# Hybrid GLA/SSD/PEER block: opening products half a round earlier, the sums' copies in another tag, and two of three passes fused in the later part of the first expert matrix

## The chip, the core and the metric

The kernel runs on one core of a Trainium2 chip: TensorE (PE, with its weight loads PEld), VectorE (DVE), ScalarE (ACT), GpSimd (POOL) and SyncE (SP), whose queue issues the large weight loads. The metric is the device time of one execution in microseconds, the median of several runs. Times inside a run come from one profiled execution.

## The reference, cut to what matters

```python
mod_x = split(silu(c) @ w_ada + b_ada, 6)            # and mod_c from c_ctx
hc = modulate(rmsnorm(ctx, norm1_w), mod_c[0], mod_c[1])
hx = modulate(rmsnorm(x, norm1_w), mod_x[0], mod_x[1])
core_c, states = branch_core(hc, 1, p, None)          # h @ w_in, then GLA and SSD scans
core_x, _ = branch_core(hx, rows, p, states)
x = x + mod_x[2] * branch_out(core_x, p)
hx2 = modulate(rmsnorm(x, norm2_w), mod_x[3], mod_x[4])
x = x + mod_x[5] * peer(hx2, peer_wq, peer_keys, peer_u, peer_v)
return rmsnorm(x, final_norm_w)
# peer: scores -> top 16 of 16384 experts per head -> softmax gates;
# act = gelu(t @ u[idx].T), y = (act * gate) @ v[idx]
```

256 latent and 256 context tokens, width 2048, one layer, everything in float32. The kernel computes the expert part densely: all 16384 rows of u against all 256 tokens, a gate matrix that is zero but for the chosen experts, and all rows of v.

## The kernel before

Every large product is done in split precision: a weight tile of 128 x 1024 arrives as `raw`, ScalarE copies it to `hi` (rounded) and VectorE computes `lo = raw - hi`; the activations are held as a pair hi/lo too. A product of one 128 x 128 slice is then three TensorE passes: Whi with the hi activations, Whi with their lo, Wlo with their hi (`mm3`, L328 to L330). `Stream` runs this supply from one plan for the whole kernel. `get` hands out the next pair, and before it does, `ahead` issues the loads up to `loads` items ahead on SyncE's queue and the splits up to `splits` ahead. There are three raw buffers (`loads - splits`) and four buffers each of hi and lo (`splits + 1`), from the first item to the last.

**The opening** (list `START`, loop at L397). The first 16 of the 24 pieces of 512 columns of the ada product stand in 8 rounds c, each of four pieces `("ada", c, i)` (`ada_piece`, 8 matmuls on four column groups, L263), whose two tiles of 512 KB each come over SyncE's queue too (`board`, up to 7 aboard, in buffers `raw0` and `s4`). After the fourth piece `ada_out` copies the sums to SBUF (ScalarE, L269; the copy is a tile of tag `s4`, five buffers, that also hold two of every seven ada tiles and two K tiles), some steps later turns them with `sel2` (TensorE, L274) and adds the bias. `h_pair(c)` then makes two slices of the modulated, normed input, hi and lo (VectorE, ScalarE). With two slices of h ready, TensorE can do the halves of v (`v_part`, L336 to L338, 12 matmuls of 512 columns each), of the low-rank and dt columns ("ld", L426 to L428, 6 matmuls each), and from round 5 a k product of 24. In round c stand v and ld of pair c - 2, four to five steps one after another between the pieces, and h of pair c - 1 behind the second piece. The engines run their queues in the order in which the code was written out; nothing reorders them.

**The first head.** Then come units of weight columns, each pass followed by `tick`, which moves every background generator by one `yield`. `gla(hd)` is one: the exponentials of a direction (`exps`), their products with Q and K (`prods`, VectorE L555 to L561), the diagonal products on TensorE (`diag`, L568), and so on. The dt stage runs on VectorE in the same stretch.

**The last sum of squares.** After the output projection, `stats` sums the squares of x1 on TensorE (L1135), and four filling ada pieces (L263) follow; the sum goes through Ln and Exp into `rs2`, and h2hi and h2lo are made slice by slice.

**The experts.** `u_tile(b, i)` multiplies a tile of 128 experts of u with h2: two gets of 8 slices each, into half a PSUM bank; every second tile Gelu reads the bank (L1374). 14 blocks of 4 tiles run alone, beside the routing. From then on each tile of the remaining 18 blocks (b of 14 to 31, `BACK = 14`) is followed by a group of v products (L1497 to L1499, 24 matmuls of 512 columns), whose sums VectorE adds to `yacc` (L1506).

Of the kernel before, what the change touches and what calls it, by code (L numbers as in the profile page):

```python
# [10 lines left out]
F32 = mybir.dt.float32  # L11
F32R = mybir.dt.float32r
U32 = mybir.dt.uint32
AF = mybir.ActivationFunctionType
OP = mybir.AluOpType
# [13 lines left out]
class Stream:  # L29
# [10 lines left out]
    def _load(self, i):  # L40
        t = self.pool.tile([P, 1024], F32, name="raw", tag="raw", bufs=self.loads - self.splits)
        self.nc.sync.dma_start(t, self.plan[i])
        self.raw[i] = t

    def _split(self, i):
        t = self.raw.pop(i)
        hi = self.pool.tile([P, 1024], F32R, name="hi", tag="hi", bufs=self.splits + 1)
        lo = self.pool.tile([P, 1024], F32R, name="lo", tag="lo", bufs=self.splits + 1)
        self.nc.scalar.activation(hi, t, AF.Copy)  # L49
        self.nc.vector.tensor_sub(lo, t, hi.bitcast(F32))  # L50
        self.done[i] = (hi, lo)
# [43 lines left out]
def hybrid_block_kernel(ctx, tc, A, out):  # L95
# [8 lines left out]
    st = Stream(nc, streams, 6, 3)  # L104

    def mmbank(shape=(P, 512)):
        return psum.tile(list(shape), F32, name="mm", tag="mm", bufs=4)
# [45 lines left out]
    START = []  # L153
    for c in range(10):
        todo = [("v", c - 2, 0), ("ld", c - 2, 0), ("v", c - 2, 1), ("ld", c - 2, 1)] if c > 1 else []
        if 4 < c < 9:
            todo.append(("k", c - 5, 0))
        for i in range(8):
            if c < 8 and i % 2:
                START.append(("ada", c, i // 2))  # L160
                if not c:
                    START.append(("norm", i // 2, 0))
            if i == 3 and 0 < c < 9:
                START.append(("h", c - 1, 0))
            if todo:
                START.append(todo.pop(0))

# [163 lines left out]

    def v_part(pv, W2, k, j):
        Whi, Wlo = W2
        for tb in range(4):
            tok = slice(P * tb, P * tb + P)
            mm_(pv[tb], Hhi[:, k, tok], Whi[:, j, :], start=k == 0, stop=False)  # L336
            mm_(pv[tb], Hhi[:, k, tok], Wlo[:, j, :], start=False, stop=False)  # L337
            mm_(pv[tb], Hlo[:, k, tok], Whi[:, j, :], start=False, stop=k == KT - 1)  # L338
# [57 lines left out]
    ada_sb = lambda: w4.tile([P, 512], F32, name="s4", tag="s4", bufs=5)  # L396
    plr = pdt = None  # L397
    Kt = {a: w4.tile([P, 2, 512], F32, name="s4", tag="s4", bufs=5) for a in range(2)}
    for k, a, b in START:
# [29 lines left out]
        else:  # L429
            pk = scbank()  # L430
            mm3(pk, st.get(), 0, 8, Hhi, Hlo, CT, True, True)
            later.append(lambda a=a, pk=pk: nc.scalar.activation(Kt[a // 2][:, a % 2], pk, AF.Copy))
        step()
    es_x.close()
    wk = es_w.enter_context(tc.tile_pool(name="wk", bufs=1, reuse_waits="tile"))
    st.limit = st.side = None
    SZ = {"s1": 256, "s2": 512, "s4": 1024}
# [84 lines left out]
    def gla(hd):  # L522
# [51 lines left out]
        yield  # L574
        diag(0)
        prods(1)
        yield
        yield
        diag(1)
# [577 lines left out]
    stats(*prev)  # L1157
    for i in range(FILL):
        ada_piece(i, fill[2 * i:2 * i + 2])
    bg.insert(0, ada_out(23))  # L1160
# [5 lines left out]
    h2hi = h2p.tile([P, KT, T], F32R, name="h2hi")  # L1166
    h2lo = h2p.tile([P, KT, T], F32R, name="h2lo")
# [192 lines left out]
    def u_tile(b, i):  # L1360
        nonlocal started
        if i % 2 == 0:
            u_tile.ps = mmbank((P, 2, 256))
        ps = u_tile.ps
        for h in range(2):
            mm3(ps[:, i % 2], st.get(), 8 * h, 8, h2hi, h2lo, slice(0, 256), h == 0, h == 1)
            if not started and not bg:
                bg.append(bg_route)
                started = True
            tick()  # L1370
        if i == 0:
            ACT_[b] = ap_.tile([P, 4, 256], F32, name="act", tag="act", bufs=BACK + 2)
        if i % 2:
            nc.scalar.activation(ACT_[b][:, i - 1:i + 1], ps, AF.Gelu)  # L1374
# [208 lines left out]
```

## Time and profile before

| | us |
|---|---|
| median of 3 runs | 3626.37 |
| lowest, highest | 3626.19, 3629.07 |
| the profiled execution | 3628.86 |
| its span, first to last instruction | 3627.1 |

Of the span TensorE is busy 3546.5 us (98%), VectorE 2368.4 (65%), ScalarE 1665.6 (46%). A matmul's busy time is longer than its distance from the next, since matmuls are pipelined; so the distance between starts says what one costs. PEclk is the clock that TensorE was granted: 1.0 is 2.4 GHz, and where the mean of a stretch is lower, part of it ran at 1.2 GHz. A wait is put down to the instruction that ended it.

### The profile page before, as it was taken

What the parts mean: (1) busy time and instruction counts of PE and PEld (TensorE: products, weight loads), DVE (VectorE), ACT (ScalarE), POOL (GpSimd) and SP (SyncE); (2) the same over time, 40 slices, a digit from 0 to 9 for tenths busy, and PEclk for the clock granted to TensorE, in tenths of its full rate; (3) what the DMA queues carried; (4) which work ended last, traced back from release to release, by engine and by line L of the source; (5) the groups of instructions that cost most, each with busy time, mean ns of one, the idle gap of its engine ahead of it and who ended that gap; (6) DMA issues with size and microseconds to landing.
All of it is one profiled execution on the core that took longest, in us unless ns stands there. A gap on an engine that the chain in (4) does not pass through costs nothing.

```text
span 3627.1 us, 58908 instructions
## 1 busy us (share of the span) xinstructions
PE 3546.5 (98%) x23679; PEld 3186.4 (88%) x23679; DVE 2368.4 (65%) x3569; ACT 1665.6 (46%) x2225; POOL 370.6 (10%) x424
## 2 busy tenths in 40 slices
PE   5989999999999999999998999999999999999998
PEld 2688899988888888999998999999999999998886
DVE  3375565777878777655545787875555555556777
ACT  2254444445555555654433446464444444444344
POOL 0000000000000000110002016360000000000004
PEclk8999999999999999999999999999999999999999
DMA  8644555655665565567666557677666666666774
GB/s 304 230 140 142 172 170 179 208 170 189 210 206 184 176 191 174 167 230 245 193 209 218 172 182 203 195 208 221 198 198 197 198 197 198 198 198 206 240 228 144
DMA packets 214145, 715.39 MB, mean 197 GB/s; under 512 B 24688, under 2 KB 24832, under 8 KB 213360
## 3 DMA queue, kind: packets, MB, share of 16 engines
q1 hardware_dynamic: 188928, 625.04, 53.5%
q0 software_dynamic: 24944, 86.59, 8.7%
q8 instruction: 186, 3.05, 0.3%
q14 instruction: 87, 0.71, 0.1%
HBM read 679.93 MB, written 31.60 MB: 196 GB/s over the span
## 4 chain that ended last, share of the span: by engine, by line
PE 92%; DVE 4%; DMA 2%; ACT 1%; issue 1%; POOL 0%; DVEq 0%; SPq 0%; ACTq 0%; POOLq 0%
PE mm L328 20%; PE mm L330 20%; PE mm L329 19%; PE mm L1498 6%; PE mm L1497 6%; PE mm L1499 6%; PE mm L336 2%; PE sc L1304 2%; PE mm L337 2%; PE mm L338 2%; DVE lo L50 1%; PE sc L875 1%; PE ad L263 1%; PE sc L615 1%; PE sc L808 1%
## 5 line engine op out<-in xcount | busy, mean ns | idle before, releaser
L50 DVE TENSOR_TENSOR lo<-raw,hi 128x1024 fp32r<-128x1024 f32 x996 | 1234.3, 1246 | 1011.8 <-ACT hi L49 1003.5
L49 ACT ACTIVATE hi<-raw 128x1024 fp32r<-128x1024 f32 x996 | 1046.0, 1058 | 1383.5 <-PE mm L329 624.5
L328 PE MATMUL mm<-Hhi,hi 128*128 128x256 f32 (+1 forms) x2272 | 737.6, 325 | 1.4 <-ACT hi L49 1.4
L330 PE MATMUL mm<-Hhi,lo 128*128 128x256 f32 (+1 forms) x2272 | 724.7, 319 | 4.0 <-DVE lo L50 4.0
L329 PE MATMUL mm<-Hlo,hi 128*128 128x256 f32 (+1 forms) x2272 | 724.2, 319 | 0.0
L328 PE MATMUL mm<-h2hi,hi 128*128 128x256 f32 x2304 | 657.7, 285 | 0.0
L329 PE MATMUL mm<-h2lo,hi 128*128 128x256 f32 x2304 | 653.1, 283 | 2.5 <-DVE h2lo L1175 2.5
L330 PE MATMUL mm<-h2hi,lo 128*128 128x256 f32 x2304 | 652.6, 283 | 0.0
L328 PEld LDWEIGHTS mm<-Hhi,hi 128*128 128x128 f32 x2272 | 435.4, 192 | 37.0 <-issue 5.3
L330 PEld LDWEIGHTS mm<-Hhi,lo 128*128 128x128 f32 x2272 | 435.2, 192 | 34.4 <-DVE lo L50 5.0
L329 PEld LDWEIGHTS mm<-Hlo,hi 128*128 128x128 f32 x2272 | 435.7, 192 | 30.3 <-issue 1.9
L329 PEld LDWEIGHTS mm<-h2lo,hi 128*128 128x128 f32 x2304 | 442.4, 192 | 6.2 <-DVE h2lo L1175 3.1
L328 PEld LDWEIGHTS mm<-h2hi,hi 128*128 128x128 f32 x2304 | 442.1, 192 | 4.1 <-ACT h2hi L1172 0.8
L330 PEld LDWEIGHTS mm<-h2hi,lo 128*128 128x128 f32 x2304 | 442.1, 192 | 0.0
L1498 PE MATMUL mm<-lo,ph 128*128 128x512 f32 x1024 | 406.1, 397 | 5.7 <-DVE lo L50 5.7
L1497 PE MATMUL mm<-hi,ph 128*128 128x512 f32 x1024 | 406.5, 397 | 0.0
L1499 PE MATMUL mm<-hi,pl 128*128 128x512 f32 x1024 | 405.1, 396 | 0.0
L1498 PEld LDWEIGHTS mm<-lo,ph 128*128 128x128 f32 x1024 | 193.0, 188 | 49.5 <-DVE lo L50 7.2
L1499 PEld LDWEIGHTS mm<-hi,pl 128*128 128x128 f32 x1024 | 193.1, 189 | 46.3
L1497 PEld LDWEIGHTS mm<-hi,ph 128*128 128x128 f32 x1024 | 193.2, 189 | 42.8
L330 PE MATMUL mm<-yh,lo 128*128 128x256 f32 x768 | 217.3, 283 | 1.0 <-DVE lo L50 1.0
L328 PE MATMUL mm<-yh,hi 128*128 128x256 f32 x768 | 217.1, 283 | 0.0
(337 smaller groups left out, 4556.1 us busy)
## 6 DMA issues: line engine op xcount, KB each, us to landing
raw<-in_w_f_dram SPq DMA_DIRECT2D x288, 512.0 KB, 3.7
raw<-in_u_dram SPq DMA_DIRECT2D x256, 512.0 KB, 4.1
raw<-in_v_dram SPq DMA_DIRECT2D x256, 512.0 KB, 4.1
ride<-in_w_ada_dram SPq DMA_DIRECT2D x240, 256.0 KB, 3.9
raw<-in_w_so_dram SPq DMA_DIRECT2D x64, 512.0 KB, 4.2
raw<-in_w_ada_dram SPq DMA_DIRECT2D x45, 512.0 KB, 7.3
raw<-in_w_v_dram SPq DMA_DIRECT2D x32, 512.0 KB, 3.6
s<-cum_d POOLq DMA_DIRECT2D x64, 256.0 KB, 6.1
```

What stands on the lines that cost most here:

```text
L49: self.nc.scalar.activation(hi, t, AF.Copy)
L50: self.nc.vector.tensor_sub(lo, t, hi.bitcast(F32))
L328: mm_(ps, Whi[:, j, :], hi[:, k, tok], start=start and j == 0, stop=False)
L329: mm_(ps, Whi[:, j, :], lo[:, k, tok], start=False, stop=False)
L330: mm_(ps, Wlo[:, j, :], hi[:, k, tok], start=False, stop=stop and j == n - 1)
L336: mm_(pv[tb], Hhi[:, k, tok], Whi[:, j, :], start=k == 0, stop=False)
L337: mm_(pv[tb], Hhi[:, k, tok], Wlo[:, j, :], start=False, stop=False)
L338: mm_(pv[tb], Hlo[:, k, tok], Whi[:, j, :], start=False, stop=k == KT - 1)
L1304: mm_(pg[:, j], o1[:, j], o2[:, j], start=True, stop=True)
L1497: mm_(ps[t, i], ghi, Whi, start=j == 0 and k == 0, stop=False)
L1498: mm_(ps[t, i], ghi, Wlo, start=False, stop=False)
L1499: mm_(ps[t, i], glo, Whi, start=False, stop=j == 1 and k == 1)
```

## The change

Five things are changed. In the opening, v and ld of pair c - 1 are put into the list behind the third piece of round c, h of pair c - 1 behind its first piece; leftover steps follow one or two at a time, and the last k product stands last. During the opening the stream loads 5 and splits 2 items ahead instead of 6 and 3, with the same numbers of buffers, and the copy of the sums takes a buffer of tag `sq1`, which the first norm has used before. In the first head, one more empty step stands before each diagonal product. The last `stats` stands behind the third of the four filling pieces. And from block 14 on a tile of u is done by `mm2`: h2hi and h2lo lie side by side in one tile `h2`, Whi multiplies both in one pass of 512 columns, Wlo the hi half in one of 256, into a whole bank, and VectorE adds the two halves of the bank before Gelu.

```diff
@@ class Stream
-        t = self.pool.tile([P, 1024], F32, name="raw", tag="raw", bufs=self.loads - self.splits)
+        t = self.pool.tile([P, 1024], F32, name="raw", tag="raw", bufs=3)
...
-        hi = self.pool.tile([P, 1024], F32R, name="hi", tag="hi", bufs=self.splits + 1)
-        lo = self.pool.tile([P, 1024], F32R, name="lo", tag="lo", bufs=self.splits + 1)
+        hi = self.pool.tile([P, 1024], F32R, name="hi", tag="hi", bufs=4)
+        lo = self.pool.tile([P, 1024], F32R, name="lo", tag="lo", bufs=4)
...
-    st = Stream(nc, streams, 6, 3)
+    st = Stream(nc, streams, 5, 2)
...
-    START = []
+    START, todo = [], []
     for c in range(10):
-        todo = [("v", c - 2, 0), ("ld", c - 2, 0), ("v", c - 2, 1), ("ld", c - 2, 1)] if c > 1 else []
-        if 4 < c < 9:
-            todo.append(("k", c - 5, 0))
-        for i in range(8):
-            if c < 8 and i % 2:
-                START.append(("ada", c, i // 2))
-                if not c:
-                    START.append(("norm", i // 2, 0))
-            if i == 3 and 0 < c < 9:
+        for i in range(4):
+            if c < 8:
+                START.append(("ada", c, i))
+            if c == 0:
+                START.append(("norm", i, 0))
+            if i == 0 and 0 < c < 9:
                 START.append(("h", c - 1, 0))
-            if todo:
-                START.append(todo.pop(0))
+            if i == 2 and 0 < c < 9:
+                todo += [("v", c - 1, 0), ("ld", c - 1, 0), ("v", c - 1, 1), ("ld", c - 1, 1)]
+                if c > 4:
+                    todo.append(("k", c - 5, 0))
+            for _ in range(2 if len(todo) > 4 else 1):
+                if todo:
+                    START.append(todo.pop(0))
+    START += todo
...
+    def mm2(ps, W2, h0, x, start, stop):
+        Whi, Wlo = (w.rearrange("p (k f) -> p k f", f=P) for w in W2)
+        for j in range(8):
+            k = h0 + j
+            last = stop and j == 7
+            for w in (Wlo, Whi) if last else (Whi, Wlo):
+                if w is Whi:
+                    mm_(ps, w[:, j, :], x[:, k], start=start and j == 0, stop=last)
+                else:
+                    mm_(ps[:, 0:256], w[:, j, :], x[:, k, 0], start=False, stop=False)
...
-    ada_sb = lambda: w4.tile([P, 512], F32, name="s4", tag="s4", bufs=5)
+    ada_sb = lambda: xp.tile([P, 512], F32, name="sq1", tag="sq1", bufs=3)
...
+            continue
+        while later:
+            later.pop(0)()
         step()
...
+    st.loads, st.splits = 6, 3
@@ gla
         yield from exps(1)
         yield
+        if hd == 0:
+            yield
         diag(0)
         prods(1)
         yield
         yield
+        if hd == 0:
+            yield
         diag(1)
...
-    stats(*prev)
     for i in range(FILL):
         ada_piece(i, fill[2 * i:2 * i + 2])
+        if i == 2:
+            stats(*prev)
...
-    h2hi = h2p.tile([P, KT, T], F32R, name="h2hi")
-    h2lo = h2p.tile([P, KT, T], F32R, name="h2lo")
+    h2 = h2p.tile([P, KT, 2, T], F32R, name="h2")
+    h2hi, h2lo = h2[:, :, 0], h2[:, :, 1]
@@ u_tile
+        wide = b >= BACK
+        if wide:
+            ps = mmbank()
...
+            if wide:
+                mm2(ps, st.get(), 8 * h, h2, h == 0, h == 1)
...
+        a = ACT_[b][:, i - 1:i + 1]
+        if wide:
+            nc.vector.tensor_reduce(ACT_[b][:, i], ps.rearrange("p (s t) -> p t s", s=2), axis=AX.X, op=OP.add)
         if i % 2:
-            nc.scalar.activation(ACT_[b][:, i - 1:i + 1], ps, AF.Gelu)
+            nc.scalar.activation(a, a if wide else ps, AF.Gelu)
```

The order of the instructions at three places follows, of before and of the changed kernel apart. Line numbers of the changed kernel are its own (L263 is L266 there, L555 L575).

SyncE's queue in rounds 1 and 2 of the opening, before. `raw<-in_w_v_dram`, `in_w_ld_dram` and `in_w_f_dram` are items of the stream (v, ld, k), all others tiles of the ada matrix, in order of their pieces:

```order
L42 DMA raw<-in_w_v_dram 128x1024
L42 DMA raw<-in_w_ld_dram 128x1024
L42 DMA raw<-in_w_v_dram 128x1024
L64 DMA s_256<-in_w_ada_dram 128x1024
L64 DMA s_258<-in_w_ada_dram 128x1024
L64 DMA raw_269<-in_w_ada_dram 128x1024
L64 DMA raw_271<-in_w_ada_dram 128x1024
L64 DMA raw_288<-in_w_ada_dram 128x1024
L64 DMA raw_290<-in_w_ada_dram 128x1024
L64 DMA raw_296<-in_w_ada_dram 128x1024
L64 DMA s_298<-in_w_ada_dram 128x1024
L42 DMA raw<-in_w_f_dram 128x1024
```

The same place in the changed kernel:

```order
L42 DMA raw<-in_w_v_dram 128x1024
L42 DMA raw<-in_w_ld_dram 128x1024
L64 DMA s_250<-in_w_ada_dram 128x1024
L64 DMA s_252<-in_w_ada_dram 128x1024
L64 DMA raw_274<-in_w_ada_dram 128x1024
L64 DMA raw_276<-in_w_ada_dram 128x1024
L64 DMA raw_282<-in_w_ada_dram 128x1024
L64 DMA raw_284<-in_w_ada_dram 128x1024
L42 DMA raw<-in_w_v_dram 128x1024
L64 DMA raw_308<-in_w_ada_dram 128x1024
L64 DMA s_310<-in_w_ada_dram 128x1024
L42 DMA raw<-in_w_v_dram 128x1024
```

Two instead of three items stand ahead of the two `s` tiles of round 1's last piece, and the following items come one by one between the ada tiles.

VectorE in the first head, before: the products of direction 0 (L555 to L561), the small factors of direction 1 (L534 to L536), splits (`lo`), the products of direction 1:

```order
L558 TENSOR_TENSOR s_1562<-s_1562,s_154 128x512
L559 TENSOR_TENSOR s_1565<-s_1565,s_154 128x256
L561 TENSOR_SCALAR s_1566<-s_1563,s_1557 128x128 x2
L534 TENSOR_SCALAR s_1659<-s_1173 128x2x2
L535 TENSOR_SCALAR s_1659<-s_1173 128x2x2
L536 TENSOR_SCALAR s_1659<-s_1173 128x2
L50 TENSOR_TENSOR lo<-raw,hi 128x1024 x2
L555 TENSOR_TENSOR s_1665<-s_1665,s_1455 128x512
```

The same place in the changed kernel:

```order
L578 TENSOR_TENSOR s_1562<-s_1562,s_154 128x512
L579 TENSOR_TENSOR s_1565<-s_1565,s_154 128x256
L581 TENSOR_SCALAR s_1566<-s_1563,s_1557 128x128 x2
L554 TENSOR_SCALAR s_1659<-s_1172 128x2x2
L555 TENSOR_SCALAR s_1659<-s_1172 128x2x2
L556 TENSOR_SCALAR s_1659<-s_1172 128x2
L50 TENSOR_TENSOR lo<-raw,hi 128x1024 x3
L575 TENSOR_TENSOR s_1665<-s_1665,s_1455 128x512
```

One split more stands ahead of the products of direction 1; on TensorE four passes of 24 instead of three stand between the dt stage's transposes and the first diagonal product, three instead of two ahead of the second.

VectorE at a tile of u in the late blocks, before, between two sums of v (`yacc`); in the second group of each block the gates of the next one (L1395, L1398) stand between too:

```order
L1506 TENSOR_TENSOR yacc<-yacc,mm 128x512 x2
L50 TENSOR_TENSOR lo<-raw,hi 128x1024 x4
L1506 TENSOR_TENSOR yacc<-yacc,mm 128x512 x2
L50 TENSOR_TENSOR lo<-raw,hi 128x1024 x2
L1395 TENSOR_TENSOR act<-act,Gb 128x1024
```

The same place in the changed kernel:

```order
L50 TENSOR_TENSOR lo<-raw,hi 128x1024 x2
L1407 TENSOR_REDUCE act<-mm 128x256
L50 TENSOR_TENSOR lo<-raw,hi 128x1024 x2
L1541 TENSOR_TENSOR yacc<-yacc,mm 128x512 x2
L50 TENSOR_TENSOR lo<-raw,hi 128x1024 x2
L1407 TENSOR_REDUCE act<-mm 128x256
L1430 TENSOR_TENSOR act<-act,Gb 128x1024
```

The addition of the two halves of the bank stands behind the second split of each tile and ahead of the splits of the v items.

## Rows read from the trace of the kernel before

**Rows 1.** The page: span, TensorE's busy time with its count, and the chain that ended last by engine.

```profile
span 3627.1 us, 58908 instructions
...
PE 3546.5 (98%) x23679; PEld 3186.4 (88%) x23679; DVE 2368.4 (65%) x3569; ACT 1665.6 (46%) x2225; POOL 370.6 (10%) x424
...
PE 92%; DVE 4%; DMA 2%; ACT 1%; issue 1%; POOL 0%; DVEq 0%; SPq 0%; ACTq 0%; POOLq 0%
```

**Rows 2.** The table by stage: stretch, length, then busy us (instructions) of PE, PEld, DVE, ACT, POOL, the granted clock, the DMA engines' busy share and GB/s. The first 150 us, and a stretch of the late blocks.

```profile
0.00:150.00 150.00, 112.86 (x544) 60.50 (x545) 51.01 (x87) 39.22 (x55) 7.49 (x18) 0.92 0.79 299
...
2700.00:2900.00 200.00, 200.00 (x1272) 180.96 (x1271) 117.42 (x115) 82.68 (x83) 2.11 (x4) 1.00 0.64 196
```

**Rows 3.** TensorE's waits in the first 330 us: who ended them, us in total, times, longest.

```profile
PE ad L263 <- DMA s<-in_w_ada_dram: 8.9, 1, 8.9
...
PE sc L568 <- DVE s L558: 4.5, 2, 3.8
...
PE mm L330 <- DVE lo L50: 3.1, 3, 2.2
PE sc L492 <- DVE s L487: 1.7, 1, 1.7
```

**Rows 4.** The waits of SyncE's queue in the first 200 us, the two longest.

```profile
SPq L42 <- DVE lo L50: 59.3, 12, 20.5
SPq L42 <- DVE s L309: 57.0, 7, 14.1
```

**Rows 5.** The chain of waits in order of time (start, us, what), pieces between 42 and 94 us: an ada tile's load, the pieces that it let start, the first piece of round 4, a turn of the sums.

```profile
42.34 6.50 DMA s<-in_w_ada_dram
48.88 3.13 PE ad L263 x8
...
92.89 0.99 PE ad L263 x8
93.88 0.98 PE sc L274 x8
```

**Rows 6.** TensorE's groups from 39 to 93 us, by shape: the first of the three lines of v and of ld.

```profile
L336 PE MATMUL mm<-hi,Hhi 128*128 128x512 f32 x20 | 8.7, 434 | 0.0
...
L426 PE MATMUL sc<-Hhi,hi 128*128 128x512 f32 x8 | 3.9, 486 | 0.0
```

**Rows 7.** The table by stage in steps of 10 us, columns as in rows 2.

```profile
20.00:30.00 10.00, 7.31 (x26) 1.42 (x22) 3.46 (x5) 4.20 (x8) 0.00 (x0) 0.93 1.03 420
...
40.00:50.00 10.00, 1.12 (x4) 0.19 (x4) 6.03 (x11) 1.36 (x3) 0.00 (x0) 0.61 0.90 317
50.00:60.00 10.00, 10.00 (x47) 6.12 (x46) 1.23 (x1) 1.54 (x2) 0.00 (x0) 0.88 0.97 375
...
250.00:260.00 10.00, 8.52 (x58) 8.38 (x59) 6.65 (x15) 6.45 (x15) 0.00 (x0) 0.83 0.45 139
```

**Rows 8.** VectorE's timeline (start, us) at the first pair of h: the bias added to the sums, and the lo parts.

```profile
41.85 0.16 DVE L279 TENSOR_TENSOR mods<-sc,b_ada 128x8 f32<-128x8 f32 x1
...
43.67 1.34 DVE L318 TENSOR_TENSOR Hlo<-xc,Hhi 128x512 fp32r<-128x512 f32 x2
```

**Rows 9.** VectorE's timeline in the first head: the reciprocal of the dt stage, the last product that the first diagonal waits for, and a split.

```profile
196.37 3.35 DVE L674 RECIPROCAL s<-s 128x512 f32<-128x512 f32 x1
...
249.90 0.69 DVE L558 TENSOR_TENSOR s<-s,s 128x512 f32<-128x512 f32 x1
...
256.01 1.23 DVE L50 TENSOR_TENSOR lo<-raw,hi 128x1024 fp32r<-128x1024 f32 x1 [3.35 <-ACT hi L49]
```

**Rows 10.** The timeline at the last sum of squares: the square, h2hi of the first slice, the first matmul with it.

```profile
1985.54 0.63 ACT L1153 ACTIVATE x1q<-x 128x512 f32<-128x512 f32 x1 [2.13 <-DVE x L1147]
...
1990.17 0.51 ACT L1172 ACTIVATE h2hi<-x,mods 128x256 fp32r<-128x256 f32 x1 [0.49 <-DVE x L1171]
...
1990.85 0.38 PE L328 MATMUL mm<-h2hi,hi 128*128 128x256 f32 x1
```

**Rows 11.** TensorE's timeline, first and last of runs of matmuls without a wait: 17 with 512 columns of h (weights of the stream) at 331.76 to 335.39; 10 with 256 columns of h2 at 2798.85 to 2799.93; 13 of the v groups, with 512 columns of the streamed tile, at 2800.04 to 2802.84.

```profile
331.76 0.39 PE L328 MATMUL mm<-Hhi,hi 128*128 128x512 f32 x1
...
335.39 0.39 PE L329 MATMUL mm<-Hlo,hi 128*128 128x512 f32 x1
...
2798.85 0.28 PE L330 MATMUL mm<-h2hi,lo 128*128 128x256 f32 x1
...
2799.93 0.28 PE L330 MATMUL mm<-h2hi,lo 128*128 128x256 f32 x1
...
2800.04 0.40 PE L1497 MATMUL mm<-hi,ph 128*128 128x512 f32 x1
...
2802.84 0.40 PE L1497 MATMUL mm<-hi,ph 128*128 128x512 f32 x1
```

**Rows 12.** Groups of VectorE and ScalarE: the two splits, the sum of v from PSUM, a reduction of the routing, and Gelu (the last from 2500 to 3400 us).

```profile
L50 DVE TENSOR_TENSOR lo<-raw,hi 128x1024 fp32r<-128x1024 f32 x996 | 1234.3, 1246 | 1011.8 <-ACT hi L49 1003.5
L49 ACT ACTIVATE hi<-raw 128x1024 fp32r<-128x1024 f32 x996 | 1046.0, 1058 | 1383.5 <-PE mm L329 624.5
...
L1506 DVE TENSOR_TENSOR yacc<-yacc,mm 128x512 f32<-128x512 f32 x240 | 153.4, 681 | 0.0
...
L1262 DVE TENSOR_REDUCE tok<-eq 128x64 f32<-128x1024 f32 x8 | 9.7, 1208 | 0.0
...
L1374 ACT ACTIVATE act<-mm 128x512 f32<-128x512 f32 x35 | 20.9, 598 | 67.9 <-PE mm L330 67.9
```

More of the change, by code (lines that the diff above doesn't have):

```diff
@@ L1361, in u_tile @@
         nonlocal started
-        if i % 2 == 0:
-            u_tile.ps = mmbank((P, 2, 256))
-        ps = u_tile.ps
+        wide = b >= BACK
+        if wide:
+            ps = mmbank()
+        else:
+            if i % 2 == 0:
+                u_tile.ps = mmbank((P, 2, 256))
+            ps = u_tile.ps
         for h in range(2):
-            mm3(ps[:, i % 2], st.get(), 8 * h, 8, h2hi, h2lo, slice(0, 256), h == 0, h == 1)
+            if wide:
+                mm2(ps, st.get(), 8 * h, h2, h == 0, h == 1)
+            else:
+                mm3(ps[:, i % 2], st.get(), 8 * h, 8, h2hi, h2lo, slice(0, 256), h == 0, h == 1)
             if not started and not bg:
```

## The prediction

> **What bounds the kernel now.** I read the page first. The span is 3627.1 us, TensorE is busy in 98% of it, and 92% of the chain that ended last is TensorE's [rows 1]. So time is to be had from TensorE's idle stretches, from its stretches at half clock, and from its own matmuls, and from nothing else. The table by stage shows where: 37 us of the first 150 us are idle, at a mean clock of 0.92, while a late stretch of the expert matrices has 200.00 busy of 200.00 us, with VectorE at 117 [rows 2]. The list of TensorE's waits in the first 330 us names who ended them [rows 3]. Behind two of those names stands another: SyncE's queue waited 116 us in the first 200 for splits (VectorE's lo and its neighbour in order) before it could issue the next weight load, with up to 20.5 us at a stretch, and the tiles of the ada matrix stand in the same queue behind it [rows 4].
>
> **Part 1, the opening (order of the products, the shorter look-ahead, the sums' copies in another tag).** From 39.98 us (48.88 less the wait of 8.9) TensorE works to the first piece of round 4 at 92.89, 52.9 us [rows 3, 5]. In that time it does 9 ada pieces of 0.99, 2 turns of the sums of 0.98 [rows 5], 60 matmuls of the v halves (20 on each of three lines) and 24 of the ld halves [rows 6], each 0.227 apart ((335.39-331.76)/16) [rows 11]. That is 8.9 + 2.0 + 13.6 + 5.4 = 29.9 us. So 23.0 us are lost, in waits for ada tiles and in the half clock behind them: in the 10 us with the long wait the granted clock is 0.61 [rows 7].
>
> What the change does to the cause, read from the code: before, get k issues the load of item k+6, which waits for the raw buffer that the split of item k+3 frees; with four hi/lo buffers that split needs the pair of item k-1, which a later v or ld half often still reads. So the queue stood until TensorE came round to that half, and the ada tiles behind it stood too. With two splits ahead the load is item k+5, the split k+2, and the pair that of item k-2, whose readers are done. The two tiles that ended the 8.9 us wait left at 42.34 and took 6.50 [rows 5]; in the new order only two weight loads, not three, stand ahead of them, and one split (some 1.2 us) less, so they land about 47.5. The first v half now stands ahead of that piece. It needs the first pair of h: its VectorE steps from the sum to the second lo part run from 41.85 to 45.01, and one split less lets them start 1.2 us sooner [rows 8]; v needs only the first half of the pair, so it starts at about 42.7. At half clock (12 x 0.454 = 5.4) it ends at 48.1, the piece behind it at half clock at 50.0. By 50.0 TensorE has lost 10.0 - 2.7 - 1.0 = 6.3 us, and if it then ran through, 23.0 - 6.3 = 16.7 us would be gained.
>
> Does the DMA allow that? A round takes 9.5 tiles of 0.524 MB, 5.0 MB; TensorE's round is 4 x 0.99 + 0.98 + 36 x 0.227 = 13.1 us. At the 375 GB/s of 50 to 60 us the tiles take 13.3 us, at the 420 of 20 to 30 us 11.9, at the 317 of 40 to 50 us 15.7 [rows 7]. So transfers are now about as long as the products. At 317, three rounds lose 2.6 us each and 9 us of gain are left, at 420 nearly 17. I take **13 us**, by the 375 and some waits; bounds 8 and 17. The later rounds have a k product more each and are TensorE's. Copies of the sums in the other tag cost nothing themselves: the same copy on ScalarE, and norm1, which used those buffers, is done by then.
>
> **Part 2, the first head.** Two things move here. The last product of the opening is now k, not v and ld, so the evacuation of v, the first splits and the dt stage start up to 5.5 us (24 x 0.227) sooner against TensorE. From the reciprocal at 196.37 VectorE runs without a gap; what it does is what TensorE waits for at L492 (1.7 us) and at the lo splits (3.1) [rows 3, 9]. But a split in front of the reciprocal still waits for a hi buffer of the first unit, so I count about half of it, **2.7 us**. The second is an empty step more before each diagonal product. The first of them waits 3.8 us for L558, which ends at 250.59; a pass of 24 matmuls (24 x 0.120 = 2.9 us) now stands ahead of it, so the wait falls to 0.9. The second waits 0.7 now. It gets another pass ahead of it, but in the new order VectorE has one split more (1.23 us) to do before it [rows 9], so I reckon it at 1.6 us later in time with two passes (5.8 us) more done: 4.2 us in all, rounded to **3.8**. Bounds of the part: 2 us if VectorE sets the time all the way, 10 if all waits and the half clock of 250 to 260 (0.83, some 1.7 us) go [rows 3, 7]. The later end of the first head is covered: a v product of 5.4 us hides its norm, and the copies of v come at most about 1 us later.
>
> **Part 3, the last sum of squares.** TensorE waits until the square ends at 1986.17, and now fills that wait with three ada pieces. But the first product of the next matrix needs h2hi, which is ready at 1990.68, and it starts at 1990.85: the chain square, sum, Ln, Exp, scale, h2hi does not move [rows 10]. The idle moves to behind the last piece: **0.2 us**, bounds 0 and 1.5.
>
> **Part 4, the fused passes.** For 18 of 32 blocks, 4 tiles, 2 halves and 8 slices, 1152 times, three passes of 256 columns become one of 512 and one of 256. The columns stay 768. A pass of 256 is 0.120 apart ((2799.93-2798.85)/9), one of 512 with the same kind of weights and a resident moving operand 0.227; the 512 passes of the second expert matrix, whose moving operand is the streamed tile, take 0.2333 ((2802.84-2800.04)/12) [rows 11]. So 0.360 becomes 0.347 or 0.353: 15.0 or 7.7 us. The nearest row is the 0.227, with the same weights' tiles and an operand held like h2; I take **14 us**, bounds 7 and 15. By these rows a pass has a fixed part of 2 x 0.120 - 0.227 = 0.013 us, and that is what is saved.
>
> The Trainium skill (TensorE: Matmul & The Clock Gate, Back-to-back issue gap) gives a warm matmul N/2.4 + 2.5 ns, so one pass fewer would save 2.5 ns; the rows here show 13, so I hold to them. By the page this part would come to an estimated 2.9 us.
>
> What part 4 adds is 72 reductions of 512 columns on VectorE. None stands in the trace; the nearest are the sum from PSUM at 0.681 and a reduction of twice the columns at 1.208 [rows 12], so 0.6 to 0.7 us each. They cost nothing: VectorE is 59% busy in that stage [rows 2], and the reduction falls where VectorE waits for a hi of ScalarE that waits for the same matmul. Behind it stand the Gelu, the next hi and the next lo, about 0.1 + 0.7 + 0.6 + 1.06 + 1.25 = 3.7 us [rows 12], against three split items of 2.8 us ahead of TensorE. If that cover were gone, each us of wait per tile would cost 72 us.
>
> **The sum.** 13 + 6.5 + 0.2 + 14 = 33.7 us. The profiled execution took 3628.86 (its span 3627.1 and 1.8 around it), 2.5 above the median of 3626.37. Against its own time that is 3595.2; against the median 3592.7, and this is the forecast, **3593**.
>
> **Rivals.**
> 1. The opening becomes the DMA's. Its queue is freed, but at the 317 GB/s of 40 to 50 us 9 us of gain are left, and one wait of some half of the old 8.9, for a weight load behind a split and that behind a copy of ScalarE, leaves 4 instead of 13: 3602. For it: products and transfers are about equal in length. Against: 375 and 420 were reached.
> 2. The fixed part of a pass is mostly weight loading that the longer pass does not save, and the pair takes 0.357: 2.9 us of 14, time 3604. Against: 0.120 and 0.227. This is also where the rule above leads.
> 3. Both: 3613.
> 4. The change does little anywhere (the waits only change their names): 3619 to 3627.
> 5. Slower. A split two ahead instead of three comes late at every get of the opening: 16 gets (8 v, 4 ld, 4 k), each with a hi of 1.06 and a lo of 1.25 [rows 12], are 37 us in place of the 13 gained, 3643. It decides as soon as ScalarE holds a split behind a sum's copy until TensorE needs it. Against: between a split and its use two gets pass, most of a round of 13 us.
>
> **How the numbers follow.** The forecast has 0.68, with its own range 3583 to 3606 from the bounds of the parts; rival 1 has 0.12, rival 2 0.09, rival 3 0.03, rival 4 0.03, rival 5 0.05. Some 0.2% (7 us) is what a measurement of this kernel can tell from no change, so faster is below 3619: 0.68 + 0.12 + 0.09 + 0.03 = 0.92, same 0.03, slower 0.05. The range 3583 to 3607 holds the forecast but for 0.07 and rivals 1 and 2, and leaves out 0.18.
>
> **What would show it.** Right: the list of waits of the first 200 us without the 8.9, SyncE's waits for lo at a fraction of 116 us, the first piece of round 4 near 77 to 80 us, matmuls 0.227 and 0.120 apart in turn in the late tiles, group by group 0.2 us shorter (16 x 0.0125), and 72 reductions at 0.6 to 0.7. Wrong: waits for ada tiles on TensorE between 50 and 100 us (rival 1), 0.237 for the wide pass (rival 2), L50 as the releaser of TensorE at each get of the opening (rival 5), or TensorE idle in the late stage, behind the reduction.

## The result and the profile after

The changed kernel takes 3601.0 us (3599.5 to 3603.8, 4 runs) against 3626.3 us of the kernel before on the same chip: ratio 0.993, 95% interval 0.9918 to 0.9943. It is 25.3 us faster where 33.7 were forecast. The time lies within the range, 8 us above the point. The profiled execution took 3603.8.

The page of the changed kernel, against [rows 1]:

```profile
span 3601.9 us, 56678 instructions
...
PE 3536.4 (98%) x22527; PEld 3123.3 (87%) x22527; DVE 2413.1 (67%) x3641; ACT 1667.3 (46%) x2225; POOL 371.7 (10%) x424
```

There are 1152 matmuls fewer on TensorE, as the fused passes want. Its share stays 98%, so what was won was TensorE's own time. The table by stage (columns as in [rows 2]) shows where it came from:

```profile
0.00:150.00 150.00, 123.98 (x625) 69.36 (x626) 57.96 (x101) 43.23 (x60) 8.09 (x19) 0.97 0.85 320
40.00:50.00 10.00, 6.88 (x22) 3.90 (x23) 5.30 (x11) 2.55 (x4) 0.00 (x0) 0.83 0.94 356
250.00:260.00 10.00, 8.80 (x66) 8.03 (x65) 6.90 (x10) 6.57 (x9) 0.00 (x0) 1.00 0.80 276
2700.00:2900.00 200.00, 200.00 (x997) 167.37 (x996) 131.03 (x135) 85.47 (x86) 2.65 (x5) 1.00 0.66 200
```

In the first 150 us TensorE is busy for 124.0 us, not 112.9, and the mean granted clock is 0.97, not 0.92 [rows 2]; the slice with the long wait is at 0.83, not 0.61 [rows 7]. The late stage has no idle time before or after. TensorE's waits in the first 330 us, and below them those of SyncE's queue in the first 200:

```profile
PE ad L266 <- DMA s<-in_w_ada_dram: 18.7, 3, 17.5
PE mm L333 <- DVE lo L50: 6.1, 5, 2.2
PE mm L352 <- ACT Hhi L319: 2.6, 1, 2.6
```

```profile
SPq L42 <- DVE lo L50: 63.5, 17, 10.8
SPq L64 <- PE ad L266: 51.7, 18, 5.6
```

The 8.9 us wait of [rows 3] is gone; what is left of the ada waits is the 17.5 us before the first piece, which the kernel before had too (18.1 us, put down there to a copy on ScalarE), and 1.2 us in two. In its place stand 2.6 us for the first h. SyncE's queue, which stood 116 us for splits [rows 4], stands 63.5 us for them and 51.7 us for ada pieces, that is for TensorE itself. Of the 116 us it is the 57.0 put down to the first step of an h pair (L309) that went, 1.0 us being left; those put down to lo were 59.3 us and are 63.5, the longest 10.8 and no longer 20.5. The waits for dt and the diagonal products (L492, L568) are gone, and waits for lo have grown from 3.1 to 6.1 us.

The late tiles, in TensorE's timeline. First a stretch of a fused tile, then passes of a v group:

```profile
2720.33 0.40 PE L344 MATMUL mm<-h,hi 128*128 128x512 f32 x1
2720.57 0.28 PE L346 MATMUL mm<-h,lo 128*128 128x256 f32 x1
2720.69 0.40 PE L344 MATMUL mm<-h,hi 128*128 128x512 f32 x1
2720.93 0.28 PE L346 MATMUL mm<-h,lo 128*128 128x256 f32 x1
2721.04 0.40 PE L344 MATMUL mm<-h,hi 128*128 128x512 f32 x1
2721.27 0.28 PE L346 MATMUL mm<-h,lo 128*128 128x256 f32 x1
2721.39 0.40 PE L344 MATMUL mm<-h,hi 128*128 128x512 f32 x1
...
2710.86 0.40 PE L1532 MATMUL mm<-hi,ph 128*128 128x512 f32 x1
2711.09 0.40 PE L1533 MATMUL mm<-lo,ph 128*128 128x512 f32 x1
2711.32 0.40 PE L1534 MATMUL mm<-hi,pl 128*128 128x512 f32 x1
2711.56 0.40 PE L1532 MATMUL mm<-hi,ph 128*128 128x512 f32 x1
2711.79 0.40 PE L1533 MATMUL mm<-lo,ph 128*128 128x512 f32 x1
```

Three pairs take 1.06 us, 0.353 each; over the whole stage the mean pair is 0.3523. That is 0.007 less than three passes of 0.1197, not 0.0125. The group of the new reductions, and Gelu behind them:

```profile
L1407 DVE TENSOR_REDUCE act<-mm 128x256 f32<-128x512 f32 x71 | 49.1, 692 | 32.8 <-PE mm L344 32.6
L1409 ACT ACTIVATE act<-act 128x512 f32<-128x512 f32 x36 | 22.8, 633 | 94.1 <-DVE act L1407 94.1
```

### The profile page after: what moved, and what is told of

Same layout as the page of the kernel before. It is cut to its first block, busy times and chain, and to the rows that moved or that the text cites. A ratio compares the mean times of both kernels' runs of the same rounds, so it can differ in the third digit from the quotient of the medians.

```text
span 3601.9 us, 56678 instructions
## 1 busy us (share of the span) xinstructions
PE 3536.4 (98%) x22527; PEld 3123.3 (87%) x22527; DVE 2413.1 (67%) x3641; ACT 1667.3 (46%) x2225; POOL 371.7 (10%) x424
## 4 chain that ended last, share of the span: by engine, by line
PE 91%; DVE 4%; DMA 3%; ACT 1%; issue 1%; SPq 0%; POOL 0%; DVEq 0%; ACTq 0%; POOLq 0%
PE mm L331 15%; PE mm L333 15%; PE mm L332 15%; PE mm L344 7%; PE mm L1533 6%; PE mm L1534 6%; PE mm L1532 6%; PE mm L346 4%; PE mm L352 2%; PE sc L1329 2%; PE mm L353 2%; PE mm L354 2%; DVE lo L50 1%; PE sc L899 1%; PE ad L266 1%
## 5 line engine op out<-in xcount | busy, mean ns | idle before, releaser
L344 PE MATMUL mm<-h,hi 128*128 128x512 f32 x1152 | 412.5, 398 | 0.0
L331 PE MATMUL mm<-h,hi 128*128 128x256 f32 x1152 | 332.1, 288 | 2.4 <-ACT h L1197 2.4
L332 PE MATMUL mm<-h,hi 128*128 128x256 f32 x1152 | 327.4, 284 | 2.2 <-DVE h L1200 2.2
L333 PE MATMUL mm<-h,lo 128*128 128x256 f32 x1152 | 327.0, 284 | 0.0
L346 PE MATMUL mm<-h,lo 128*128 128x256 f32 x1152 | 312.1, 281 | 0.0
L344 PEld LDWEIGHTS mm<-h,hi 128*128 128x128 f32 x1152 | 216.6, 188 | 49.4
L1534 PEld LDWEIGHTS mm<-hi,pl 128*128 128x128 f32 x1024 | 192.8, 188 | 46.5
L1532 PEld LDWEIGHTS mm<-hi,ph 128*128 128x128 f32 x1024 | 192.7, 188 | 43.5 <-issue 0.3
L331 PEld LDWEIGHTS mm<-h,hi 128*128 128x128 f32 x1152 | 222.1, 193 | 3.3 <-ACT h L1197 3.3
L332 PEld LDWEIGHTS mm<-h,hi 128*128 128x128 f32 x1152 | 222.2, 193 | 2.9 <-DVE h L1200 2.9
```

Source lines behind the costliest of these rows:

```text
L331: mm_(ps, Whi[:, j, :], hi[:, k, tok], start=start and j == 0, stop=False)
L332: mm_(ps, Whi[:, j, :], lo[:, k, tok], start=False, stop=False)
L333: mm_(ps, Wlo[:, j, :], hi[:, k, tok], start=False, stop=stop and j == n - 1)
L344: mm_(ps, w[:, j, :], x[:, k], start=start and j == 0, stop=last)
L346: mm_(ps[:, 0:256], w[:, j, :], x[:, k, 0], start=False, stop=False)
L1532: mm_(ps[t, i], ghi, Whi, start=j == 0 and k == 0, stop=False)
```

## The experiments

To compare parts, I cut every trace at the same six instructions: the first ada matmul, the first product of the units, the first v product of the second head, the last matmul of the output projection, the 241st matmul with h2, and TensorE's last. The differences of their starts, in us:

| kernel | median | opening | first head | to the output projection | around part 3 | rest |
|---|---|---|---|---|---|---|
| before | 3626.3 | 167.5 | 91.1 | 1704.7 | 45.5 | 1590.7 |
| changed | 3601.0 | 152.4 | 86.2 | 1705.2 | 46.6 | 1584.9 |
| look_only | 3611.9 | 152.8 | 90.0 | 1703.6 | 46.8 | 1590.3 |
| open_only | 3608.2 | 151.9 | 88.1 | 1702.8 | 46.2 | 1589.7 |
| no_yields | 3603.7 | 150.8 | 89.1 | 1703.2 | 46.3 | 1583.5 |
| stats_back | 3598.4 | 152.2 | 85.3 | 1703.3 | 45.6 | 1583.4 |
| no_fuse | 3605.0 | 152.9 | 85.5 | 1701.5 | 45.9 | 1589.7 |
| fuse_all | 3617.5 | 150.9 | 85.4 | 1703.4 | 46.5 | 1601.6 |
| align | 3592.4 | 153.6 | 85.3 | 1703.0 | 45.8 | 1576.6 |
| align512 | 3583.7 | 150.7 | 86.3 | 1702.8 | 46.5 | 1566.4 |
| align512_no_fuse | 3589.3 | 152.6 | 84.8 | 1702.1 | 45.4 | 1575.7 |
| runs_of_2 | 3576.1 | 152.4 | 86.2 | 1702.9 | 45.5 | 1563.2 |
| runs_of_8 | 3576.4 | 153.2 | 86.2 | 1700.3 | 46.6 | 1561.0 |
| runs8_plain | 3593.9 | 150.8 | 86.3 | 1702.7 | 46.0 | 1579.9 |

The same code differs by up to 3 us in the opening, 5 in the long middle and 1.2 around part 3 from one trace to another, so a term is read from groups of rows, not from one pair. Of the kernel before and of each experiment there is one trace. The medians come from several chips, on which the kernel before took 3624.9 to 3627.3 us, so a difference of two medians is uncertain by about 2 us too.

**open_only**: the kernel before with part 1 alone.

> The kernel before with part 1 alone (the opening's list, 5 pieces and 2 splits ahead, the sums' copies in another tag, the copies of k after the next entry). Theory (opening milestones of the two traces: 15.1 us): 3610 to 3612 us. Rival (part of the 15 us is given back in the first head, whose waits the later parts remove): 3614 to 3618 us. Forecast term was 13 us: 3613 us.

Measured 3608.2 us (ratio 0.9949, 0.9935 to 0.9963). Opening and first head together are 18.6 us shorter; the theory is 2 us short, the rival of a gain given back is out.

**look_only**: of part 1 only the look-ahead, with the old list and the old tag (the numbers of buffers stay, as in the changed kernel).

```diff
-    st = Stream(nc, streams, 6, 3)
+    st = Stream(nc, streams, 5, 2)
```

> The kernel before with only the look-ahead of the opening at 5 pieces and 2 splits, its old list kept. If the 8.9 us wait at 48.9 us goes away by the look-ahead alone, the first product of the units starts 10 us or more earlier than before (185.6 us); if the order of the list does it, within 3 us of before.

Its waits and slices: one row of TensorE's waits, one of SyncE's, two of the table by stage, and last 50 to 80 us, first of the kernel before, then of this one:

```profile
PE ad L263 <- DMA s<-in_w_ada_dram: 24.8, 2, 17.4
...
SPq L42 <- DVE lo L50: 80.2, 17, 19.4
...
40.00:50.00 10.00, 4.43 (x11) 1.51 (x12) 3.08 (x5) 2.46 (x4) 0.00 (x0) 0.51 0.96 357
50.00:60.00 10.00, 10.00 (x54) 6.51 (x54) 6.55 (x11) 2.55 (x4) 0.00 (x0) 0.97 1.00 386
...
50.00:80.00 30.00, 28.98 (x138) 16.77 (x137) 6.74 (x12) 5.41 (x7) 0.00 (x0) 0.90 0.70 263
...
50.00:80.00 30.00, 30.00 (x166) 18.14 (x169) 13.52 (x23) 7.86 (x11) 0.00 (x0) 0.99 0.94 348
```

A single run: 3611.9 us, and the opening is 14.7 us shorter, nearly all of what the whole part gives (15.5 as the mean of the twelve kernels that have it). Neither expectation fits: the wait did not go (24.8 less the first 17.4 leaves 7.4 us), and yet the time came. Most of it came behind the wait, which ends at 45.6 us (48.9 before): from 50 us on TensorE has no wait, and its clock in the next 10 us is 0.97, where the kernel before had 0.88 [rows 7] and then two more waits (1.0 and 3.8 us, ending at 70.8 and 86.1). In those 30 us the DMA engines moved 263 GB/s before and move 348 here: the loads of the ada tiles leave earlier. SyncE's queue still stands 80.2 us for lo, 19.4 us at the longest; what went is the 57.0 us for L309 (1.0 left). What the prediction had read from the code, a split that needs a pair which a v half still reads, stands in ScalarE's waits from 20 to 165 us, of the kernel before, of this one and of the changed kernel (L338 and L354 are the last matmul of a v step):

```profile
ACT hi L49 <- PE mm L338: 37.9, 4, 12.1
...
ACT hi L49 <- PE mm L338: 5.4, 3, 1.8
...
ACT hi L49 <- PE mm L354: 1.9, 4, 0.5
```

The new list fills the wait with the first half of the first v product, of which six of twelve passes run at half clock (0.43 us apart), and ends the opening less than 1 us sooner, which is less than what traces differ by. The new list or the other tag without the shorter look-ahead was not run, so whether they alone would have done it too is not known.

**no_yields**: the changed kernel without the two empty steps (`if hd == 0: yield`, twice).

> The changed kernel without the two empty steps of the first head. Theory (the kernel with part 1 alone starts the v product of the second head 2 us later than kernels with parts 1 and 2): 2 us more than the changed kernel, 3603 us, with a wait of 4 to 5 us ahead of the first diagonal product. Forecast (3.8 us of the part's 6.5 are the empty steps): 3605 us.

Measured 3603.7 us (ratio 0.994, 0.9926 to 0.9953), 2.7 more than the changed kernel. The wait is back, as the theory has it:

```profile
PE sc L588 <- DVE s L578: 5.0, 2, 4.4
```

In the table no_yields and open_only have a first head of 88.6 on average, the ten kernels with the steps 85.8: 2.8 us.

**stats_back**: the changed kernel with `stats(*prev)` ahead of the loop again.

> The changed kernel with part 3 undone: the last sum of squares ahead of the four fill pieces again. Theory (the part moved the idle time behind the fill, gaps of 2.39, 0.81 and 1.12 us after it, and lengthened the half clock from 3.4 to 6.8 us): about 1 us less than the changed kernel, 3600 us; a gap of 3.6 us ahead of the sum, half clock one slice of 3.4 us. Forecast (the part gains 0.2 us): 3601.2 us. A median can hardly tell the two apart; the time from the last matmul of the output projection to a matmul 30 us later can.

Measured 3598.4 us (ratio 0.9925, 0.9908 to 0.9941). The 10 us around the first products with h2 (1970 to 1980 us in both), first of the changed kernel, then of this one:

```profile
1970.00:1980.00 10.00, 7.21 (x31) 6.52 (x32) 10.00 (x22) 6.21 (x14) 4.07 (x5) 0.67 0.01 2
...
1970.00:1980.00 10.00, 8.61 (x63) 7.59 (x62) 9.66 (x24) 7.23 (x15) 2.41 (x4) 1.00 0.00 0
```

These two traces alone (46.6 and 45.6 in the table) would say that part 3 costs 1 us. The groups of rows do not: the four kernels with the old order have 45.5 to 46.8 there (mean 46.0), the ten with the new one 45.4 to 46.6 (mean 46.1). My theory is not borne out; the half clock falls differently from trace to trace, and the part is worth nothing that these traces can tell.

**no_fuse**: the changed kernel without part 4 (`wide = False`).

> The changed kernel without part 4 (three passes per piece of u everywhere, Gelu from PSUM). Theory (the trace after: a pair of 0.3529 us for 3 x 0.1197 us, 6.1 ns x 1152 = 7.0 us, of which 5.7 came out): 3606 to 3608 us, 5 to 7 us over the changed kernel. Rival (part 4 gave its forecast 14 us and something else in the late stage took 8 back): about 3601 us with that other loss still in it, or 3615 us if the loss belongs to the passes.

Measured 3605.0 us (ratio 0.9942, 0.9928 to 0.9955), 4.0 above the changed kernel. In the rest column the four kernels without fused passes and with the old place of v's weights have 1590.1 on average, the three with them 1583.9: part 4 gives 6.2 us, and the rival is out: no other loss of 8 us stands against it.

**fuse_all**: fused passes in all 32 blocks (`wide = True`).

> The changed kernel with fused passes in all 32 blocks of u, so that 896 more pairs run in a stage where no group of v stands between them. Theory A (a pass of 512 columns takes 0.235 us after one of 256, wherever it stands): 6.1 ns x 896 = 5.5 us less, 3595.5 us, pairs of 0.353 us in blocks 0 to 13 too. Theory B (the late stage slows passes of 512 columns, and the early blocks run at the 0.227 us of the projections): pairs of 0.344 to 0.347 us in blocks 0 to 13, 11 to 14 us less, 3587 to 3590 us. Rival C (the reductions on VectorE collide with the search for the largest scores, whose stage has VectorE busy): 3601 us or more, with waits of TensorE for PSUM.

Measured 3617.5 us (ratio 0.9974, 0.9964 to 0.9984): 16.5 us slower than the changed kernel, as rival C has it, though the waits are not for PSUM. The two largest of TensorE's waits from 2005 to 2460 us (18.3 us in all, where the changed kernel has one of 0.8 us), and a row of the table by stage:

```profile
PE sc L1318 <- DVE tok L1287: 9.3, 2, 4.7
PE mm L346 <- DVE lo L50: 4.9, 6, 1.6
...
2100.00:2200.00 100.00, 90.50 (x518) 77.69 (x517) 85.11 (x161) 45.15 (x50) 26.14 (x23) 0.97 0.52 164
```

VectorE is 85% busy there with the search for the largest scores, as in the changed kernel, which has no reductions there; with 0.69 us more a tile TensorE waits for the routing's sums and for lo. The pairs that had no wait took 0.349 to 0.351 us on average, by stretch; in the late blocks the mean is 0.3523, and the median 0.350 in both. So the price of a pair is not one of the late stage, and theory B is out.

**align** and **align512**: a small buffer of the last stage padded, which moves the weights of the v groups. In the changed kernel ph and pl start 32 bytes past a multiple of 512; here 64, and 0, as the slices of Hhi do. No operand of the fused passes moves; the buffers of the gates (Gb, read by VectorE) and of the last block move along with ph and pl.

```diff
-    ssq = vp.tile([P, 2, 4], F32, name="ssq")
+    ssq = vp.tile([P, 2, 8], F32, name="ssq")[:, :, 0:4]
...
+    ssq = vp.tile([P, 2, 64], F32, name="ssq")[:, :, 0:4]
```

> The changed kernel with the last stage's small buffer ssq padded from 32 to 64 bytes per partition, which moves the weights of the v groups (ph, pl) from addresses 32 bytes past a multiple of 64 to multiples of 64, like Hhi in the projections. Theory P (the place of an operand makes the 0.2333 us of a v pass out of the 0.227 us of the projections): 3072 passes x 6.6 ns = 20 us less, 3581 us, passes of v at 0.227 us. Theory S (it is the stage, or what runs beside it): no change, 3601 us, passes of v at 0.2333 us.

> The changed kernel with the last stage's small buffer padded to 512 bytes per partition, so that every 128-column weight slice of the v groups begins at a multiple of 512 bytes, as the slices of Hhi in the projections do (padded to 64 bytes in the run before, where the passes of v stayed at 0.2333 us and the fused pairs fell from 0.3523 to 0.347). Theory P' (a slice's place on 512 bytes decides between 0.2267 and 0.2333): passes of v at 0.227 us, 3072 x 6.6 ns = 20 us less than that run, some 3572 us. Rival S (the stage decides): passes of v stay at 0.233, pairs of 0.347 or 0.352, 3592 to 3601 us.

align took 3592.4 us (ratio 0.9904, 0.9889 to 0.9919). A stretch of its pairs, and its v passes:

```profile
2714.13 0.39 PE L344 MATMUL mm<-h,hi 128*128 128x512 f32 x1
...
2716.21 0.39 PE L344 MATMUL mm<-h,hi 128*128 128x512 f32 x1
...
2717.59 0.39 PE L1532 MATMUL mm<-hi,ph 128*128 128x512 f32 x1
...
2722.49 0.39 PE L1532 MATMUL mm<-hi,ph 128*128 128x512 f32 x1
```

The passes of v stayed at 0.2333 ((2722.49 - 2717.59)/21), but the pairs fell to 0.347 ((2716.21 - 2714.13)/6), which neither theory had. align512 took 3583.7 us (0.9887, 0.9871 to 0.9904): its v passes, and a stretch of its pairs,

```profile
2715.19 0.39 PE L1534 MATMUL mm<-hi,pl 128*128 128x512 f32 x1
2715.42 0.39 PE L1532 MATMUL mm<-hi,ph 128*128 128x512 f32 x1
...
2719.95 0.39 PE L1534 MATMUL mm<-hi,pl 128*128 128x512 f32 x1
2720.18 0.39 PE L344 MATMUL mm<-h,hi 128*128 128x512 f32 x1
...
2720.52 0.40 PE L344 MATMUL mm<-h,hi 128*128 128x512 f32 x1
...
2722.64 0.40 PE L344 MATMUL mm<-h,hi 128*128 128x512 f32 x1
```

are 0.2267 apart ((2719.95 - 2715.19)/21), and the pairs 0.353 again ((2722.64 - 2720.52)/6). So the weights' place makes 0.2333 out of 0.2267, theory P'; the 3572 us were missed because the pairs went back. The pair's price does not follow that place in the same way: 0.352, 0.347 and 0.352 us at 32, 64 and 0 bytes.

**align512_no_fuse**: align512 with `wide = False`.

> The same place of the v weights, without part 4. If the pair costs 0.347 us with the v weights well placed, part 4 is worth (0.359 - 0.347) x 1152 = 14 us here, the forecast's own figure: 14 us over the run with the fused passes in the same place. If the pair's price has nothing to do with the place: 4 to 6 us over it, as without the padding (3605 against 3601).

Measured 3589.3 us (ratio 0.9902, 0.9886 to 0.9919): 5.6 above align512 by the medians, 9.3 by the rest column, not 14. With v's weights on 512 bytes the pair does not come back to 0.347.

**runs_of_2**, **runs_of_8**: align512 with two, or eight, passes of 512 columns in a row and then as many of 256 (in the last half of a tile, the short ones first). **runs8_plain**: eight and eight with the old place.

```diff
-        for j in range(8):
-            k = h0 + j
-            last = stop and j == 7
+        for j0 in range(0, 8, 8):
+            last = stop and j0 + 8 == 8
             for w in (Wlo, Whi) if last else (Whi, Wlo):
+                for j in range(j0, j0 + 8):
+                    k = h0 + j
...
```

> The changed kernel with the v weights on multiples of 512 bytes and the fused passes in another order: two of 512 columns, then two of 256, instead of one and one. Theory Q (changing from a pass of one length to one of the other costs; the pair's 0.352 us stands in a cycle of three pairs that long and short in turn bring about): half as many changes, pairs of about 0.349 us, 3 us less than with 512 bytes alone, some 3581 us. Rival R (0.352 is what a 512 and a 256 pass take here, in any order): 0.352 and 3584 us.

> The same with eight passes of 512 columns, then eight of 256. Theory Q: 0.227 and 0.120 as in unmixed runs, 0.347 a pair, 1152 x 0.0055 = 6 us less, 3577 us. Rival R: 3584 us.

> The changed kernel with its own place of the v weights, and eight passes of 512 columns, then eight of 256. Theory Q (the pair's excess is the change of length): pairs at 0.347 us but for a few passes behind each change, 4 to 6 us less than the changed kernel, 3595 to 3597 us, and with it part 4 at 10 to 12 us of its forecast 14. Rival (the passes of 512 columns take 0.233 us in this stage unless the v weights lie on 512 bytes): 0.353 a pair, 3601 us.

They took 3576.1 (ratio 0.9861, 0.9844 to 0.9877), 3576.4 (0.9862, 0.9846 to 0.9879) and 3593.9 us (0.9911, 0.9896 to 0.9926). By the rest column that is 3.2 and 5.4 us less than align512, where theory Q had 3 and 6, and 4.0 less than the 1583.9 of the old place, where it had 4 to 6; a whole tile takes 0.348 to 0.349 us a pair in all three. Theory Q holds for these layouts, rival R is out, and the first two beat both kernels, by 50 and 25 us. In runs_of_8 the timeline puts equal passes into one line; the end of a tile, and the next one up to its last passes:

```profile
2711.54 2.00 PE L345 MATMUL mm<-h,hi 128*128 128x512 f32 x8
2713.38 0.39 PE L1533 MATMUL mm<-hi,ph 128*128 128x512 f32 x1
...
2718.82 1.98 PE L345 MATMUL mm<-h,hi 128*128 128x512 f32 x8
2720.63 2.08 PE L347 MATMUL mm<-h,lo 128*128 128x256 f32 x16
2722.55 0.63 PE L345 MATMUL mm<-h,hi 128*128 128x512 f32 x2
```

Eight passes of 512 columns behind the v group take 1.81 us (0.226 each), sixteen of 256 take 1.92 (0.120), and eight of 512 behind passes of 256 take 1.84. Start to start, in cycles at 2.4 GHz, that last run reads 562, 566, 547, 559, 554, 542, 545, 542: the change from short to long costs 68 cycles over 544 a pass, 28 ns, spread over five passes. With one and one in turn it is paid at every pair in part: the changed kernel reads 578, 288, 566, 271, 559, 281 and again from the front.

## Why the prediction was right, and where it was off

**Part 1 (13 us forecast): 15.5 us.** Right in sign and cause: SyncE's queue stood for a split whose buffer came late, and the shorter look-ahead freed it; look_only shows that the look-ahead alone brings 14.7 us, and takes the waits of the splits for v halves from 37.9 to 5.4 us. The sign for it in SyncE's waits came by half: of 116 us of waits 64.5 are left, and those put down to lo are not fewer. The first piece of round 4 starts at 79.1 us, where 77 to 80 were forecast and 92.8 stood before. What I had wrong is the account within the 16.7: I credited the list with filling the long wait (6.3 us left of 10.0), and the list adds under 1 us to the look-ahead. That half of what it fills in runs at half clock may be the reason; this was not tried apart. The choice of 13, by 375 GB/s, was low: the transfers kept up (415 and 414 GB/s in the two slices from 50 to 70 us), and TensorE has no ada wait behind 50 us. Rival 1 and rival 5 (splits too late) did not come.

**Part 2 (6.5): 5.4 us.** The empty steps give 2.8, not 3.8 (the working itself had 4.2, and put it down as 3.8 without a reason). The other 2.5, as against 2.7, came with part 1; look_only, with the old list, has 1.1 of them, so they are not all the k product's. The diagonal waits went as forecast, but 3 us of waits for lo grew in their place, the bound "if VectorE sets the time".

**Part 3 (0.2): nothing that shows** (0.1, with a spread of 1.2).

**Part 4 (14): 6.2 us. This step failed.** Its sentence was "The nearest row is the 0.227, with the same weights' tiles and an operand held like h2". Both prices that it took for a long pass were rows of unmixed runs. The runs show three things in its place. The 0.2333 of the v groups, which I had as the other end, goes by where their weights lie, and has nothing to do with h2. The unmixed 0.227 does hold for h2 (runs_of_8). And long and short passes in turn, the order of the change, cost 0.3523 us a pair in the changed kernel's layout, where the sum of both is 0.2267 + 0.1197 = 0.3464: 1152 x 0.0059 = 6.8 of the 7.8 us missing. The last 1.0 is within what the rest column differs by. The order alone is not the cause: align has the same order at 0.347 a pair, and its rest column is 1590.1 - 1576.6 = 13.5 us below the kernels without fused passes, with v at the same 0.2333. So whether the change got 6 or 14 us hung on where buffers happened to lie; why it does stays open. In runs of eight at the good place the part gives 1575.7 - 1561.0 = 14.7 us, the forecast's size. The lower price, 0.353 and so 7.7 us, was nearly it, but by accident.

Rival 2 gave 0.357 a pair for the reason that the fixed part is not saved; the measured 0.352 lies between it and the forecast's 0.347, but its reason is out, since the fixed part is saved in unmixed runs. Its sign, 0.237 for the wide pass, nearly came (0.236 on average), but the short pass behind it takes 0.117 instead of 0.120. The rule of the Trainium skill (TensorE: Matmul & The Clock Gate, Back-to-back issue gap), N/2.4 + 2.5 ns for a single warm matmul, came to an estimated 2.9 us; no kernel here agrees, its 215.8 ns for 512 columns standing against 226.7 at best.

The reductions were forecast at 0.6 to 0.7 and are 0.692, hidden in the late stage as argued; fuse_all shows the price where that cover is gone.

The sum: 15.5 + 5.4 + 6.2 = 27.1 against the 25.3 of the medians. That the time lies only 8 us off is in part luck, since part 1 gave 2.5 us more than forecast. (The bounds of the parts add up to 17 and 43.5 us, so to 3609 and 3583; the 3606 is not their sum.) The trace of the changed kernel itself has 15.1 + 5.0 - 0.5 - 1.1 + 5.8, and 0.6 us before the first matmul, 25.0 by the unrounded numbers. What of the 2 us between the two is chance in the middle (1705.2, the longest of all) was not tried.

## What to carry to other kernels

A price for an instruction taken from a run of equal instructions is safe for such a run only: where a change puts long and short matmuls in turn, look for a row with that order, or make runs of each. Before calling a pass slow "by its stage", look at where its operands lie; a 480-byte pad gave more than the fused passes did. And when a queue stands, ask what its oldest load is waiting for: a smaller number of items ahead, alone, gave nearly all that the whole new opening gives.

## What the hardware showed that I had not expected

- With the same columns and type, a pass of 512 in the v groups takes 226.7 ns (544 cycles) if its 128-column weights start on a multiple of 512 bytes (align512), and 233.3 (560) at 32 or 64 bytes past one (changed kernel, align). Other places, and the moving operand's, were not tried. The place is not all: v products of the opening, with weights on such multiples and at full clock, take 226.6 to 232.7 ns a pass (changed kernel, from 53 us on). The Trainium skill (TensorE: Matmul & The Clock Gate, Step-by-step: what each phase is for) says that weights have a read port of their own and take no bandwidth from the running matmul; no run here looks at the ports, and the 6.6 ns stand beside it.
- A change from 256 to 512 columns costs 28 ns over five passes (runs_of_8). One and one in turn settles in one of two cycles: 0.352 us a pair (changed kernel, align512) or 0.347 (align, where only buffers of the last stage lie elsewhere: the v weights between the tiles, the gates, the last block's). Why a tile stays in the cycle that it is in stays open.
